# Gather of experts: the sample block as one tile of 64 rows, a 23rd weight block, a permuted product

## Chip, cores, metric

One core of a Trainium2 chip. The time is that of the device, in microseconds, from start to end of one execution; it is given as the median of three runs.

## What is computed

One layer of a decoder for a prompt of 512 tokens and a sample group of 8 x 4 = 32 tokens, in float32: attention, convolution and memory branches, their sum `x1`, and on it a mixture of 32 experts. Only that last part is touched:

```
def hier_moe(h, lw):
    ...
    gates = jnp.einsum('nk,nke->ne', w, jax.nn.one_hot(expert_ids, N_EXPERTS, dtype=jnp.float32)).astype(h.dtype)
    y = jnp.zeros_like(h)
    for e in range(N_EXPERTS):
        hid = jax.nn.silu(h @ lw['w_expert_gate'][e]) * (h @ lw['w_expert_up'][e])
        y = y + gates[:, e:e + 1] * (hid @ lw['w_expert_down'][e])
    return y
```

Each token goes to two of the 32 experts (the best group of 8, two experts in it). An expert's weights are 1024 x 512 (gate), 1024 x 512 (up) and 512 x 1024 (down).

## The kernel before

The branches and the output projection fill the first 710 us; nothing of them is changed. Then the router's result is turned into tables, and the experts follow one after the other, 0 to 31.

**Tokens.** They lie in five blocks `xts[0..4]` of 128 rows by 1024 columns: four of prompt rows, and block 4 with the 32 sample rows (copied there from `x1s`, 32 rows of which lie in each of four groups of partitions, lines 1136 to 1138) and zeros below. `posE` holds for each row and expert the place of the row in the expert's list, at most `CAP` = 64 rows; further ones go to a loop for overflow behind the 32 experts.

**Gather.** An expert's 64 rows are picked by matmuls with one-hot matrices (`gather`, line 1290). So that this can be done in float16, `to_halves` (line 1323) turns each block into a high half (ScalarE, `nc.scalar.mul`) and a low half (VectorE, the rest). A gather runs over 5 blocks x 2 halves x 2 halves of the columns, 20 matmuls. The result is copied by ScalarE to `xg` (line 1298), transposed in four pieces (line 1301) and scaled by VectorE into `xT1` (line 1302). Expert 0's input `xT0` is made ahead of the halves, in float32 (lines 1336 to 1353).

**An expert** (`expert_mm`, line 1471): gate and up products (line 1477, 32 matmuls each in the profile), behind them the gather for the next expert (`mid`), then silu on ScalarE, the product `hs` on VectorE (line 1486), two transposes of it, with columns taken in steps of two (line 1489), a copy to `hT` (line 1491), the down product (line 1495), the scaling by the gates (line 1498) and a scatter with addition by GpSimd (line 1499).

**Weights.** Each expert has six loads of 1024 KB: gate, gate, up, up, down, down. I number them 0 to 191; loads 6e to 6e + 5 belong to expert e. They are all issued in this order by SyncE's queue (`wload`, line 1430; line 573 in the profile), and load n also waits for load n - 4. Their blocks come in rounds from seven pools (`mraw`, line 1414): ring2 4, ring2b 2, ring2c 1, ring 6, ring3 5, ring4 2, ring5 2, so 22 in all:

```
        q = seq[0] % (RING + RING2 + RING2B + RING2C + RING3 + RING4 + RING5)
        for cand, n in ((ring2, RING2), (ring2b, RING2B), (ring2c, RING2C), (ring, RING), (ring3, RING3), (ring4, RING4), (ring5, RING5)):
```

Load n takes the block of load n - 22 and waits until the last matmul that reads it is over. The pool ring holds places 7 to 12 of each round, ring4 18 and 19, ring5 20 and 21; ring5 takes memory that the router's tables held.

**Overflow tables.** In the program behind expert 14's loads stands `overflow_tables` (line 1503). Its work memory `scr` is a block of the pool ring too, the next one in turn. In the fourth round, loads 66 to 87, ring holds loads 73 to 78; `scr` takes the block of load 73. Its instructions on VectorE begin at line 1522; line 1530 writes the number of overflow blocks, `novf`. The read of that number by the engines (line 1576) is written behind the last expert, but the scheduler, which orders every engine's instructions by times that it works out itself, puts SyncE's read between load 84 and load 85. SyncE's queue stops there until line 1530 is done.

Of the kernel before, what the change touches and what calls it, by code (L numbers as in the profile page):

```python
# [11 lines left out]
F32 = mybir.dt.float32  # L12
# [5 lines left out]
ALU = mybir.AluOpType  # L18
# [3 lines left out]
P = 128  # L22
D = 1024
NP = 512
NS = 32
# [11 lines left out]
CAP = 64  # L37
# [14 lines left out]
RING2B = 2  # L52
RING2C = 1
RING3 = 5
RING4 = 2
RING5 = 2
SPOS = 2
NPG = 2
# [95 lines left out]
def build(tc, I, O, cols):  # L154
    nc = tc.nc
# [25 lines left out]
    ident = cp.tile([P, P], F32, name="ident")  # L181
# [17 lines left out]
    def nm(s):  # L199
        cnt[0] += 1  # L200
        return f"{s}_{cnt[0]}"
# [593 lines left out]
    for b in range(DB):  # L795
# [14 lines left out]
        for h in range(4):  # L810
            r = slice(32 * h, 32 * h + 32)
            q = [qm[:, 4 * g + h, :] for g in range(3)]
            nc.tensor.matmul(psA[r], q[1], KT[h], start=False, stop=last, skip_group_check=True)
        for h in range(4):
            r = slice(32 * h, 32 * h + 32)
            q = [qm[:, 4 * g + h, :] for g in range(3)]
            nc.tensor.matmul(psB[r, 0:P], q[0], KT[h][:, 384:], start=False, stop=False, skip_group_check=True)
        for h in range(4):
            r = slice(32 * h, 32 * h + 32)
            q = [qm[:, 4 * g + h, :] for g in range(3)]  # L820
# [261 lines left out]
    rh = rt.tile([P, 5], F32, name="frh")  # L1082
# [13 lines left out]
    xts = {i: x_buf(i, [P, D], F32, "x1") for i in range(5)}  # L1096
    xst = ExitStack()
    xp = xst.enter_context(pool("xs", 1, side="right"))
    x1s = xp.tile([P, 256], F32, name="x1s")
# [47 lines left out]

    nc.vector.scalar_tensor_tensor(lg[:32, 4, :], pr[:32, 4, :], rss[:32], br_[:32], op0=ALU.mult, op1=ALU.add)
    nc.gpsimd.tensor_scalar(rh[:, 4:5], rs[:, 4:5], HS, None, op0=ALU.mult)

    def scores(ip):
        a = slice(2 * ip, 2 * ip + 2)
# [62 lines left out]
    V = nc.vector  # L1215
# [74 lines left out]
    def gather(oh, psum, xg, xT):  # L1290
        px = psum()
        for i in GORD:
            parts = halves_of[i]
            for r, src in enumerate(parts):
                for f in range(2):
                    nc.tensor.matmul(px[CAP * f:CAP * f + CAP], oh[:, i, :], src[:, 4 * f:4 * f + 4, :],  # L1296
                                     start=(i == GORD[0] and r == 0), stop=(i == GORD[-1] and r == len(parts) - 1))
        nc.scalar.copy(xg, px)
        pt = psum()
        for c in range(4):  # L1300
            mark = nc.tensor.transpose(pt[:, c * P:(c + 1) * P], xg[:, c * P:(c + 1) * P], ident)
        nc.vector.tensor_tensor(xT.rearrange("p (f c) s -> p c f s", f=2),
                                pt.rearrange("p (c f s) -> p c f s", c=4, f=2),
                                gE.rearrange("p (f c) -> p c f", f=2).unsqueeze(3).to_broadcast([P, 4, 2, CAP]),
                                op=ALU.mult)
        return mark
# [8 lines left out]
    work = h2pool.tile([P, 1184], F32, name="work")  # L1315
    for i in GORD:
        picked = V.tensor_scalar(oh0[i], cfs("iota64"), posE[:, i, 0:1], rh[:, i:i + 1], op0=ALU.is_equal, op1=ALU.mult)
    xT0 = h2pool.tile([P, 8, CAP], F32, name="xT0")
    def not_before(ins, other):
        tc.add_manual_dep(ins.ins, other.ins.name,  # L1320
                          mybir.DependencyInfo(mybir.DependencyClass.Sync, mybir.DependencyReason.DATA), reason="order")

    def to_halves(i, h2, act, dve):
        src = halves_of[i][0]
        for f in range(2):
            ks = slice(4 * f, 4 * f + 4)
            with tc.issue_after(act.ins):
                act = nc.scalar.mul(h2[:, 0, ks], src[:, ks], rh[:, i:i + 1])
            if i == 4 and not f:
                not_before(act, picked)  # L1330
            with tc.issue_after(dve.ins):
                V.scalar_tensor_tensor(h2[:, 1, ks], src[:, ks], rh[:, i:i + 1], h2[:, 0, ks],
                                       op0=ALU.mult, op1=ALU.subtract)
        return [h2[:, 0], h2[:, 1]]

    mark = counted
    for v in range(2):
        px = mm.tile([P, 2, P], F32, name=nm("mm"), tag="mm")
        for i in GORD:
            for f in range(2):  # L1340
                k = 4 * v + 2 * f
                with tc.issue_after(mark.ins):
                    got = nc.tensor.matmul(px[CAP * f:CAP * f + CAP], oh0[i], halves_of[i][0][:, k:k + 2, :],
                                           start=(i == GORD[0]), stop=(i == GORD[-1]))
        mark = got
        xv = xp.tile([P, 256], F32, name="xv") if v else xT0[:, 4:].rearrange("p k s -> p (k s)")
        copied = nc.scalar.copy(xv, px.rearrange("p a b -> p (a b)"))
        pt = tr.tile([P, 2, 2, CAP], F32, name=nm("tr"), tag="tr")
        for c in range(2):
            nc.tensor.transpose(pt[:, c].rearrange("p f s -> p (f s)"), xv[:, c * P:(c + 1) * P], ident)  # L1350
        ks = slice(4 * v, 4 * v + 4)
        taken = V.tensor_tensor(xT0[:, ks].rearrange("p (f c) s -> p c f s", f=2), pt,
                        gE[:, ks].rearrange("p (f c) -> p c f", f=2).unsqueeze(3).to_broadcast([P, 2, 2, CAP]), op=ALU.mult)

    for i in (4, 0, 1, 2, 3):
        shape = [P, 2, 8, P]
        h2 = h2pool.tile(shape, F16, name=nm("h2")) if i == 4 else x_buf((i - 1) % 5, shape, F16, "h2")
        halves_of[i] = to_halves(i, h2, counts if i == 4 else copied, taken)
    xgT = x_buf(3, [P, D], F32, "xgT")
# [111 lines left out]
    def expert_mm(xT, w, gc, idc2, mid, early):  # L1471
        pgt = pm.tile([P, 256], F32, name=nm("pg"), tag="pg")
        pup = pm.tile([P, 256], F32, name=nm("pu"), tag="pu")
        for ps, ws in ((pgt, w[0:2]), (pup, w[2:4])):
            for k in range(8):
                for f in range(2):
                    last = nc.tensor.matmul(ps[CAP * f:CAP * f + CAP], xT[:, k, :], ws[k // 4][:, k % 4, 256 * f:256 * f + 256],  # L1477
                                     start=(k == 0), stop=(k == 7))
            if early is not None and ps is pgt:
                early(last)  # L1480
        if mid is not None:
            with tc.issue_after(last.ins):
                mid()
        hs = work[:, 512:768]
        nc.scalar.activation(hs, pgt, AF.Silu)
        nc.vector.tensor_tensor(hs, hs, pup, op=ALU.mult)  # L1486
        ph = pm.tile([P, 2, P], F32, name=nm("ph"), tag="ph", bufs=1)
        for k in range(2):
            nc.tensor.transpose(ph[:, k, :], hs.rearrange("p (q k) -> k p q", k=2)[k], ident)
        hT = work[:, 768:1024].rearrange("p (f s) -> p f s", f=2)  # L1490
        nc.vector.tensor_copy(hT, ph)  # L1491
        pd = pm.tile([P, 512], F32, name=nm("pd"), tag="pd")
        for kk in range(4):
            for f in range(2):
                last = nc.tensor.matmul(pd[CAP * f:CAP * f + CAP], hT[:, kk % 2, CAP * (kk // 2):CAP * (kk // 2) + CAP],  # L1495
                                 w[4 + kk // 2][:, kk % 2, 512 * f:512 * f + 512], start=(kk == 0), stop=(kk == 3))
        o = work[:, :512]
        nc.vector.tensor_scalar(o, pd, gc, None, op0=ALU.mult)  # L1498
        nc.gpsimd.indirect_dma_start(out=y2, out_offset=bass.IndirectOffsetOnAxis(ap=idc2, axis=0), in_=o,  # L1499
                                     in_offset=None, compute_op=ALU.add)  # L1500
        return last
# [142 lines left out]
```

## Time and profile before

| | |
|---|---|
| median of 3 runs | 1222.54 us (1222.43 to 1224.62) |
| profiled execution | 1223.19 us, span 1221.4 us |
| TensorE busy | 1157.7 us, 95% |
| VectorE, ScalarE, GpSimd busy | 483.6, 303.0, 290.0 us |
| read from HBM, written | 295.66 MB, 31.35 MB |
| granted TensorE clock, mean | 0.992 |

The span runs from the first to the last instruction. Times in the trace count from its start. A matmul's time in the trace is from its start to its modelled end; matmuls overlap, so the busy time of a group is less than the sum of its instructions. The share of DMA is the mean over the core's 16 DMA engines.

### The profile page before, as it was taken

The numbers are of one execution on the slowest core, as the hardware profiler recorded it, in microseconds if no ns is written. First come the engines' busy times: TensorE is split into PE (matmuls) and PEld (weight loads), VectorE is DVE, ScalarE is ACT, GpSimd is POOL, SyncE is SP. The second block draws the span as 40 slices with busy tenths as digits, with TensorE's granted clock in tenths as the row PEclk, the third lists the DMA queues.
The fourth block names the chain that finished last, engine by engine and source line by source line (L and its number), as shares of the span: only waits on it lengthen the run. The fifth ranks groups of instructions, "written<-read, shape, count | busy, mean of one in ns | idle before, by whom it ended". The sixth has DMA issues, their size and how long they took to land. (4 is left out here: it accounts for less than half of the span.)

```text
span 1221.4 us, 22282 instructions
## 1 busy us (share of the span) xinstructions
PE 1157.7 (95%) x9250; PEld 853.9 (70%) x9250; DVE 483.6 (40%) x959; ACT 303.0 (25%) x731; POOL 290.0 (24%) x472
## 2 busy tenths in 40 slices
PE   6999999999999989999999997999999999888886
PEld 5898898989645889999998853555555555444442
DVE  6634444343534879946433254211133221111111
ACT  7434344423322422244332223000000000000000
POOL 4442434540740640212222000111111111001111
PEclk9999999999999989999999998999999999999998
DMA  9994754132656643313309477999999999999996
GB/s 321 233 333 118 251 155 163 45 110 104 209 169 226 224 123 103 104 36 104 139 6 404 164 289 273 395 405 404 404 378 384 406 402 406 404 403 404 403 404 241
DMA packets 117382, 313.02 MB, mean 256 GB/s; under 512 B 12841, under 2 KB 69489, under 8 KB 92448
## 3 DMA queue, kind: packets, MB, share of 16 engines
q1 hardware_dynamic: 107248, 295.58, 64.2%
q0 software_dynamic: 7280, 14.36, 5.3%
q10 hardware_dynamic: 2752, 1.65, 0.5%
q8 instruction: 74, 1.21, 0.4%
q14 instruction: 28, 0.23, 0.1%
HBM read 295.66 MB, written 31.35 MB: 268 GB/s over the span
## 5 line engine op out<-in xcount | busy, mean ns | idle before, releaser
L1499 POOL DMA_INDIRECT out_y_all<-work,ids x32 | 49.6, 1550 | 454.5 <-DVE work L1498 428.7
L664 PE MATMUL mm<-hTh,lo 128*128 128x272 f32 x512 | 148.5, 291 | 0.0
L663 PE MATMUL mm<-hTl,hi 128*128 128x272 f32 x512 | 148.4, 290 | 0.0
L662 PE MATMUL mm<-hTh,hi 128*128 128x272 f32 x512 | 148.3, 290 | 0.0
L1477 PE MATMUL pu<-w,xgT 128*64 128x256 f32 x992 | 115.3, 381 | 15.8 <-DMA w<-in_w_expert_up 14.5
L1495 PE MATMUL pd<-w,work 128*64 128x512 f32 x512 | 119.5, 609 | 1.0 <-DVE work L1491 0.5
L1477 PE MATMUL pg<-w,xgT 128*64 128x256 f32 x992 | 114.6, 380 | 2.4 <-DMA w<-in_w_expert_gate 1.2
L238 PE MATMUL mm<-hi,hTh 128*128 128x256 f32 x384 | 110.2, 287 | 0.0
L1477 PEld LDWEIGHTS pu<-w,xgT 128*64 128x64 f32 x992 | 69.3, 137 | 58.4 <-DMA w<-in_w_expert_up 23.6
L239 PE MATMUL mm<-lo,hTh 128*128 128x256 f32 x384 | 110.0, 286 | 0.0
L240 PE MATMUL mm<-hi,hTl 128*128 128x256 f32 x384 | 109.8, 286 | 0.0
L1477 PEld LDWEIGHTS pg<-w,xgT 128*64 128x64 f32 x992 | 70.3, 137 | 53.6 <-issue 16.0
L232 DVE TENSOR_TENSOR lo<-w,hi 128x2048 fp32r<-128x2048 f32 (+2 forms) x46 | 82.2, 1803 | 45.9 <-ACT hi L231 45.9
L662 PEld LDWEIGHTS mm<-hTh,hi 128*128 128x128 f32 x512 | 96.7, 189 | 1.8 <-ACT aS L896 0.8
L1486 DVE TENSOR_TENSOR work<-work,pu 128x256 f32<-128x256 f32 x32 | 13.5, 421 | 211.5 <-PE pu L1477 211.5
L663 PEld LDWEIGHTS mm<-hTl,hi 128*128 128x128 f32 x512 | 96.8, 189 | 0.3 <-issue 0.2
L664 PEld LDWEIGHTS mm<-hTh,lo 128*128 128x128 f32 x512 | 96.3, 189 | 0.6 <-issue 0.5
L683 DVE SCALAR_TENSOR_TENSOR cT<-u,cT 128x512 f32<-128x512 f32 x120 | 89.5, 763 | 1.7
L1495 PEld LDWEIGHTS pd<-w,work 128*64 128x64 f32 x512 | 34.4, 139 | 64.5 <-issue 60.6
L1296 PE MATMUL px<-h,ohs 128*64 128x512 f16 x620 | 74.0, 380 | 5.4 <-DVE gates L1373 2.8
L231 ACT CAST hi<-w 128x2048 fp32r<-128x2048 f32 (+2 forms) x50 | 68.1, 1391 | 27.8 <-PE mm L663 24.7
L999 POOL TENSOR_TENSOR z<-z,gth 128x272 f32<-128x272 f32 x32 | 35.7, 1117 | 164.0 <-DVE gth L998 164.0
(454 smaller groups left out, 2119.7 us busy)
## 6 DMA issues: line engine op xcount, KB each, us to landing
w<-in_w_expert_gate SPq DMA_DIRECT2D x64, 1024.0 KB, 11.1
w<-in_w_expert_up SPq DMA_DIRECT2D x64, 1024.0 KB, 10.3
w<-in_w_expert_down SPq DMA_DIRECT2D x64, 1024.0 KB, 11.1
w<-in_w_in SPq DMA_DIRECT2D x30, 512.0 KB, 7.1
w<-in_w_in SPq DMA_DIRECT2D x12, 1024.0 KB, 6.5
out_k_win_sample<-in_cache_k SPq DMA_DIRECT2D x8, 1016.0 KB, 12.9
out_v_win_sample<-in_cache_v SPq DMA_DIRECT2D x8, 1016.0 KB, 15.7
w<-in_cache_k SPq DMA_DIRECT2D x6, 1024.0 KB, 6.0
```

The source lines that it names most:

```text
L231: nc.scalar.copy(hi[:, s], v8(t)[:, s])
L232: last_lo[0] = e.tensor_tensor(lo[:, s], v8(t)[:, s], hi[:, s].bitcast(F32), op=ALU.subtract)
L238: nc.tensor.matmul(ps, xh[k], wh[k], start=(k == 0), stop=False)
L239: nc.tensor.matmul(ps, xh[k], wl[k], start=False, stop=False)
L240: nc.tensor.matmul(ps, xl[k], wh[k], start=False, stop=(k == n - 1))
L662: nc.tensor.matmul(ps, wh[k], xh[k], start=(k == 0), stop=False)
L663: nc.tensor.matmul(ps, wh[k], xl[k], start=False, stop=False)
L664: nc.tensor.matmul(ps, wl[k], xh[k], start=False, stop=(k == n - 1))
L683: nc.vector.scalar_tensor_tensor(cTf[:, c, :NP], u[:, c, j:j + NP], w, cTf[:, c, :NP], op0=ALU.mult, op1=ALU.add)
L1296: nc.tensor.matmul(px[CAP * f:CAP * f + CAP], oh[:, i, :], src[:, 4 * f:4 * f + 4, :], start=(i == GORD[0] and r == 0), stop=(i == GORD[-1 ...
L1477: last = nc.tensor.matmul(ps[CAP * f:CAP * f + CAP], xT[:, k, :], ws[k // 4][:, k % 4, 256 * f:256 * f + 256], start=(k == 0), stop=(k == 7))
L1495: last = nc.tensor.matmul(pd[CAP * f:CAP * f + CAP], hT[:, kk % 2, CAP * (kk // 2):CAP * (kk // 2) + CAP], w[4 + kk // 2][:, kk % 2, 512 * ...
```

## The change

Three edits.

1. The 32 sample rows stand twice in block 4, in rows 0 to 31 and 32 to 63 (four more copies from `x1s` on GpSimd's queue). `posE` of block 4 is copied to rows 32 to 63. Of the float16 tile of block 4, rows 0 to 31 hold the high halves and rows 32 to 63 the low halves, so its share of a gather is one pair of matmuls over 64 rows instead of two pairs over 128. Expert 0's own gather takes 32 rows of block 4.
2. ring4 has three blocks. `xT0` has no tile of its own any more: it lies in the first block of ring4, which becomes free when expert 0's gate and up products have read it. 23 weight blocks go round.
3. The product of silu and up is written permuted, the two groups of columns apart, into the 256 columns that held `hT`; `hT` is written where silu's result was. The transposes read contiguous columns.

```
-RING4 = 2
+RING4 = 3
...
     nc.gpsimd.tensor_scalar(rh[:, 4:5], rs[:, 4:5], HS, None, op0=ALU.mult)
+    for q in range(4):
+        nc.gpsimd.dma_start(xts[4][32:64, 256 * q:256 * q + 256], x1s[32 * q:32 * q + 32, :])
...
-                    nc.tensor.matmul(px[CAP * f:CAP * f + CAP], oh[:, i, :], src[:, 4 * f:4 * f + 4, :],
+                    nc.tensor.matmul(px[CAP * f:CAP * f + CAP], oh[:64 if i == 4 else P, i, :], src[:, 4 * f:4 * f + 4, :],
...
-    xT0 = h2pool.tile([P, 8, CAP], F32, name="xT0")
+    nc.vector.tensor_copy(posE[32:64, 4, :], posE[0:32, 4, :])
+    xT0 = ring4.tile([P, 2048], F32, name=nm("w"), tag="w")[:, :512].rearrange("p (k s) -> p k s", k=8)
...
+        a, b = (slice(0, 64), slice(32, 64)) if i == 4 else (slice(0, P), slice(0, P))
+        his = h2[a] if i == 4 else h2[:, 0]
+        los = h2[b] if i == 4 else h2[:, 1]
...
-                act = nc.scalar.mul(h2[:, 0, ks], src[:, ks], rh[:, i:i + 1])
+                act = nc.scalar.mul(his[:, ks], src[a, ks], rh[a, i:i + 1])
...
-                V.scalar_tensor_tensor(h2[:, 1, ks], src[:, ks], rh[:, i:i + 1], h2[:, 0, ks],
+                V.scalar_tensor_tensor(los[:, ks], src[b, ks], rh[b, i:i + 1], h2[b, ks] if i == 4 else his[:, ks],
                                        op0=ALU.mult, op1=ALU.subtract)
-        return [h2[:, 0], h2[:, 1]]
+        return [his] if i == 4 else [his, los]
...
-                    got = nc.tensor.matmul(px[CAP * f:CAP * f + CAP], oh0[i], halves_of[i][0][:, k:k + 2, :],
+                    rows = slice(0, NS if i == 4 else P)
+                    got = nc.tensor.matmul(px[CAP * f:CAP * f + CAP], oh0[i][rows], halves_of[i][0][rows, k:k + 2, :],
...
-        nc.vector.tensor_tensor(hs, hs, pup, op=ALU.mult)
+        hp_ = work[:, 768:1024].rearrange("p (k q) -> p k q", k=2)
+        nc.vector.tensor_tensor(hp_.rearrange("p k q -> p q k"), hs.rearrange("p (q k) -> p q k", k=2),
+                                pup.rearrange("p (q k) -> p q k", k=2), op=ALU.mult)
...
-            nc.tensor.transpose(ph[:, k, :], hs.rearrange("p (q k) -> k p q", k=2)[k], ident)
-        hT = work[:, 768:1024].rearrange("p (f s) -> p f s", f=2)
+            nc.tensor.transpose(ph[:, k, :], hp_[:, k], ident)
+        hT = hs.rearrange("p (f s) -> p f s", f=2)
```

The scheduler and the pools make more of this than the diff shows. In the rows that follow a name's number is that of its tile, `w` are weight blocks (and `scr`), DMAHW counts the landings of loads, and the lines are those of the program the rows are from.

On SyncE's queue, loads 18 to 23, before:

```order
L573 DMA w_8602<-in_w_expert_gate 128x2048 [waits DMAHW1_49,Pool_49]
L573 DMA w_8604<-in_w_expert_gate 128x2048 [waits DMAHW4_49]
L573 DMA w_8606<-in_w_expert_up 128x2048 [waits DMAHW5_49]
L573 DMA w_8608<-in_w_expert_up 128x2048 [waits DMASW3_49,DMASW4_49,DMASW2_49,DMASW5_49,DMASW1_49,DMASW6_49,DMASW0_49,DMASW7_49,DVE_49,DMAHW2_49,PE_49,DMAHW6_49,Activation_49,Pool_49]
L573 DMA w_8610<-in_w_expert_down 128x2048 [waits DMAHW7_49,DMAHW3_49,PE_49]
L573 DMA w_8612<-in_w_expert_down 128x2048 [waits DMAHW0_49,PE_49]
```

and in the change:

```order
L573 DMA w_8601<-in_w_expert_gate 128x2048 [waits DMAHW1_49,Pool_49]
L573 DMA w_8603<-in_w_expert_gate 128x2048 [waits DMAHW4_49]
L573 DMA w_8605<-in_w_expert_up 128x2048 [waits DMAHW5_49,DVE_49,PE_49]
L573 DMA w_8607<-in_w_expert_up 128x2048 [waits DMAHW6_49,DMAHW2_49]
L573 DMA w_8609<-in_w_expert_down 128x2048 [waits DMASW5_49,DMASW4_49,DMASW6_49,DMASW3_49,DMASW7_49,DMASW2_49,DMAHW3_49,DMASW1_49,DMAHW7_49,DMASW0_49,Pool_49]
L573 DMA w_8611<-in_w_expert_down 128x2048 [waits DMAHW0_49]
```

Load 20, the first up load of expert 3, waits for TensorE now, and loads 21 to 23 stand behind it.

On VectorE, around the first instructions of the overflow tables, before (`pd` scaled in the first row is expert 11's, the product in the last is expert 12's):

```order
L1498 TENSOR_SCALAR work<-pd_9419,gates 128x512 [waits DMASW0_49,DVE_49,PE_49]
L1522 TENSOR_TENSOR w_9626<-cn,cf 128x256 [waits DMAHW2_49,DMAHW6_49,DMAHW0_49,PE_49]
...
L1530 CAST novf<-w_9626 128x1 [waits DVE_49]
L1531 TENSOR_TENSOR w_9626<-w_9626 128x32
L1533 TENSOR_TENSOR w_9626<-OH,w_9626 128x320 [waits DVE_49]
L1486 TENSOR_TENSOR work<-work,pu_9443 128x256 [waits PE_49,Activation_49]
```

and in the change (again from the scaling of expert 11 on; line 1494 is the product, 1500 the copy to `hT`, 1304 the gathered input, 1507 the scaling, 1531 the first instruction of the tables, 1539 the count):

```order
L1507 TENSOR_SCALAR work<-pd_9400,gates 128x512 [waits DMASW4_49,PE_49]
L1494 TENSOR_TENSOR work<-work,pu_9424 128x128x2 [waits PE_49,Activation_49]
L1286 TENSOR_TENSOR ohs<-posE,cf 128x320 [waits PE_49]
L1500 COPY work<-ph_9486 128x256 [waits DVE_49,PE_49]
L1304 TENSOR_TENSOR xgT_8266<-px_9478,gE 128x4x2x64 [waits PE_49]
L1531 TENSOR_TENSOR w_9603<-cn,cf 128x256 [waits DMAHW2_49,DMAHW3_49,DMAHW1_49,PE_49]
...
L1507 TENSOR_SCALAR work<-pd_9490,gates 128x512 [waits DMASW5_49,PE_49]
...
L1539 CAST novf<-w_9603 128x1 [waits DVE_49]
```

The tables stand behind four instructions of expert 12 that they stood ahead of, and expert 12's scaling stands among them, ahead of the count. SyncE's read of the count stands between loads 84 and 85 in both.

## Rows read from the trace of the kernel before

**Rows 1.** The page: the span, and the DMA line of its 40 slices.

```profile
span 1221.4 us, 22282 instructions
...
DMA  9994754132656643313309477999999999999996
```

**Rows 2.** Windows: stretch, length, busy us of PE, PEld, DVE, ACT, POOL, clock, DMA share, GB/s.

```profile
756.00:906.00 150.00, 146.72 (x1138) 80.82 (x1134) 29.19 (x54) 10.69 (x22) 15.48 (x10) 1.00 1.02 399
921.00:1030.00 109.00, 106.92 (x853) 59.37 (x850) 22.55 (x51) 7.19 (x15) 12.36 (x8) 1.00 1.02 402
1030.00:1200.00 170.00, 150.68 (x1102) 76.18 (x1104) 28.66 (x52) 10.31 (x21) 16.52 (x11) 1.00 1.02 406
```

**Rows 3.** Waits from 1030 us on: us in total, times, longest.

```profile
PE pu L1477 <- DMA w<-in_w_expert_up: 14.5, 20, 1.7
```

**Rows 4.** Timeline of the last expert's down product: start, us, engine, line.

```profile
1210.67 1.94 PE L1495 MATMUL pd<-w,work 128*64 128x512 f32 x8 [0.42 <-DMA w<-in_w_expert_down]
```

**Rows 5.** Timeline of SyncE's queue: loads 20 and 21, 22 and 23, 24 and 25, 26.

```profile
716.57 3.27 SPq L573 DMA_DIRECT2D w<-in_w_expert_up  x2
730.28 2.06 SPq L573 DMA_DIRECT2D w<-in_w_expert_down  x2
734.42 2.06 SPq L573 DMA_DIRECT2D w<-in_w_expert_gate  x2
749.71 2.64 SPq L573 DMA_DIRECT2D w<-in_w_expert_up  x2
```

**Rows 6.** Windows at the start of the experts.

```profile
720.00:760.00 40.00, 33.59 (x226) 15.92 (x224) 18.51 (x33) 13.90 (x16) 1.74 (x1) 0.91 0.73 267
744.00:750.80 6.80, 6.11 (x17) 1.80 (x17) 2.42 (x4) 1.02 (x2) 0.00 (x0) 0.51 0.05 8
```

**Rows 7.** Timeline of SyncE's queue: loads 84 and 85, and load 85 alone.

```profile
905.98 10.04 SPq L573 DMA_DIRECT2D w<-in_w_expert_gate  x2
...
915.69 0.34 SPq L573 DMA_DIRECT2D w<-in_w_expert_gate  x1
```

**Rows 8.** Waits of SyncE's queue, 900 to 920 us.

```profile
SPq L1576 <- DVE w L1531: 8.5, 1, 8.5
```

**Rows 9.** Windows: from load 84's issue to its landing.

```profile
906.00:917.40 11.40, 11.40 (x96) 6.50 (x92) 6.41 (x26) 0.56 (x2) 1.54 (x1) 1.00 0.85 314
```

**Rows 10.** Timeline of TensorE: expert 1's gate; expert 12's gate, gather, transposes, down product.

```profile
753.43 3.67 PE L1477 MATMUL pg<-w,xgT 128*64 128x256 f32 x32 [0.87 <-DVE xgT L1302]
...
907.90 3.62 PE L1477 MATMUL pg<-w,xgT 128*64 128x256 f32 x32
...
914.80 2.33 PE L1296 MATMUL px<-h,ohs 128*64 128x512 f16 x20
...
917.87 0.66 PE L1301 MATMUL px<-ident,xgT 128*128 128x128 f32 x4 [0.30 <-ACT xgT L1298]
918.56 3.65 PE L1495 MATMUL pd<-w,work 128*64 128x512 f32 x16
```

**Rows 11.** Timeline of GpSimd: the last of the four copies of x1s.

```profile
654.91 0.50 POOL L1138 DMA_DIRECT2D x<-x1s  x1 [1.85 <-DMA out_y_all<-x]
```

**Rows 12.** Timeline of VectorE: the overflow tables up to the count, expert 12's scaling.

```profile
911.57 0.43 DVE L1522 TENSOR_TENSOR w<-cn,cf 128x256 f32<-128x256 f32 x1 [2.70 <-PE pg L1477]
...
914.01 0.17 DVE L1527 COPY w<-w 128x8 f32<-128x8 f32 x1
...
914.59 0.15 DVE L1530 CAST novf<-w 128x1 int32<-128x1 f32 x1
...
922.39 0.74 DVE L1498 TENSOR_SCALAR work<-pd,gates 128x512 f32<-128x512 f32 x1
```

**Rows 13.** DMA issues, KB, us to landing: load 26, load 84, load 85, each in a window of its own.

```profile
w<-in_w_expert_up SPq DMA_DIRECT2D x1, 1024.0 KB, 5.0
w<-in_w_expert_gate SPq DMA_DIRECT2D x1, 1024.0 KB, 11.4
w<-in_w_expert_gate SPq DMA_DIRECT2D x1, 1024.0 KB, 5.4
```

More of the change, by code (lines that the diff above doesn't have):

```diff
@@ L1355, in build @@
     for i in (4, 0, 1, 2, 3):
-        shape = [P, 2, 8, P]
+        shape = [P, 8, P] if i == 4 else [P, 2, 8, P]
         h2 = h2pool.tile(shape, F16, name=nm("h2")) if i == 4 else x_buf((i - 1) % 5, shape, F16, "h2")
```

## The prediction

> **What bounds the kernel now.** I read the page first: the span and the DMA line of the forty slices [rows 1]. From about 760 us on the DMA digit is 9 almost everywhere, while TensorE too looks full. The windows tell the two apart [rows 2]: from 756 to 906 us TensorE is busy 146.72 of 150 us and the DMA share is 1.02; from 1030 to 1200 us the share is still 1.02, but TensorE is down to 150.68 of 170 us. The waits of that late stretch name what it lacks: up-weights, 20 waits [rows 3]. So TensorE starts with a stock of weights loaded ahead, uses it up until about 1030 us, and then lives from hand to mouth. All through this the weight stream is the bound, and the last load sets the end: the second half of the last down product begins at 1210.67 us, released by its load, and only 1.94 us of matmuls, a scaling and one scatter follow [rows 4]. **A gain on TensorE is therefore worth nothing by itself; only what stops or restarts the weight stream counts.** It stops in two places, and I read both.
>
> The first is the start. With 22 blocks, loads 20 and 21 go out at 716.57 us; load 22 needs the block of expert 0's first gate half and goes at 730.28, loads 24 and 25 need its up halves (734.42, the second at about 736.2), load 26 its first down half (749.71) [rows 5]. Between these the stream runs dry: 8 GB/s in 744 to 750.8 us, and 267 GB/s over 720 to 760 us, so 10.7 MB moved [rows 6].
>
> The second is in the middle. SyncE's queue issues load 84 at 905.98 us and load 85 only at 915.69 [rows 7]. The waits say why: 8.5 us for VectorE, at the read of the overflow count (L1576), which stands in the queue between loads 84 and 85 [rows 8]. In this stretch the DMA share is 0.85 [rows 9]: 0.15 x 11.4 us = 1.7 us are lost even now.
>
> **Part by part.** *One tile of 64 rows for the sample.* Each gather loses 2 of its 20 matmuls, which take 2.33 us together [rows 10]: 0.233 us. The rest of the cycle keeps its length: TensorE waits 0.30 us for ScalarE's copy before the transposes [rows 10], and that copy starts when the gather ends, so all of it shifts. From expert 1's gate at 753.43 to expert 12's at 907.90 us the cycle is 154.47 / 11 = 14.04 us; it becomes 13.81. Behind the weight stream this is worth nothing, but it brings forward, by 12 x 0.233 = 2.8 us, the moment of expert 12's down product, which is needed below. The conversion to halves keeps its instructions (fewer partitions, the same 512 columns), so I leave the start of expert 1 where it is. The copy of 32x32 positions on VectorE lies in the gap in which VectorE waits for the first gather. The four added x1s copies on GpSimd take about 0.50 us each [rows 11], behind waits for earlier copies to land; rh and the sample's logits follow some 3 us later, but VectorE now takes the logits two instructions later, so nothing waits. Without that cover it would be the same 3 us, once, on a stretch in which TensorE is full. They add 0.13 MB at a time when the stream has a dry spell ahead of it.
>
> *The permuted product.* The transposes read contiguous columns. They stand between the gather and the 0.30 us wait for ScalarE [rows 10], so what they save lengthens that wait: nothing. The product itself runs under the gather of the next expert (2.10 us after the change); only above that would it show, and then behind the weight stream.
>
> *The 23rd block at the start.* Expert 0's input lies in the first block of ring4, so load 20 now waits for expert 0's last up matmul, about 736.2 us, with loads 21 and 22 behind it although ring5 is free. The stream is dry from about 723 us (loads 20 and 21 no longer fill 723 to 728). But then seven loads (20 to 26) may go at once, and the next block falls free at 749.7, before they are done: the dry spell of 744 to 750.8 is gone. Moved by 760 us: 3 us before 723, and from 737.4 (the issue and 1.2 us) 22.6 us, at 406 GB/s [rows 2]: 10.4 MB against 10.7. That is 0.3 MB, 0.7 us: no difference, within one us either way, and it doesn't reach the end, since the second stop absorbs it.
>
> *The 23rd block in the middle: the term that decides.* The overflow tables (L1522 to L1530, then L1531 on) work in a block taken from ring, the next in its turn. Their first instruction waited for the last reader of load 73, half of expert 12's gate, and ran at 911.57 us, when that gate product ended [rows 12]. With 23 blocks the round of four begins at load 69 instead of 66, ring's six places hold loads 76 to 81, and the block next in turn is that of load 76: expert 12's first down half. The order of VectorE's instructions shows it too: product, transposed copy and gathered input of expert 12 now stand ahead of the first table instruction, and the scaling of expert 12's down product stands between it and the count. SyncE's read of the count has kept its place, ahead of load 85. So:
> - expert 12's down product starts at 918.56 - 2.8 = 915.8 us and is half done after 3.65 / 2 us [rows 10]: 917.6 us, the first table instruction;
> - twelve instructions, 911.57 to 914.01 before [rows 12], 2.44 us: 920.0 us. The down product is over by then (919.4), so the scaling (0.74 us) ends at 920.8 us;
> - the last five up to the count, 914.01 to 914.59 + 0.15 = 914.74 before: 921.5 us;
> - from the count's end to load 85's issue it was 915.69 - 914.74 = 0.95 us: **922.4 us**.
>
> By then the four loads in flight have landed (load 84 took 11.4 us from 905.98, so 917.4) and the queue is empty. A load into an empty queue landed after 5.0 us (load 26) and load 85 itself after 5.4 [rows 13]. So load 85 lands at 922.4 + 5.0 = 927.4 us instead of 915.69 + 5.4 = 921.1: **+6.3 us**. [...]
>
> From there the stream is full again as before, and every later load and the end move by the same amount. TensorE can't win it back: its stock is smaller, so it meets the stream some experts after 12 and not at 1030 us.
>
> **The sum.** PE gain 0, start 0 (absorbed), middle +6.3. The profiled execution took 1223.19 us with a span of 1221.4 and lies 0.65 above the median of 1222.54, so 1229.5 on its scale and **1228.8 us** as a median. Bounds: if TensorE's cycle lost the 0.30 us wait as well, the count came 3.6 us earlier: +2.7, 1225.2. If the 2.8 us of TensorE don't come: +9.1, 1231.6. That gives 1225.0 to 1232.0.
>
> **Rivals.**
> - *The table's start is not pushed back, and the change is not slower.* Then the count comes 2.8 us earlier than before, SyncE no longer stops long enough to empty the stream, and the 1.7 us come back: 1220.8 us. It decides at a count ready by about 916 us. For it: only the 2.8 us. Against: the block's number and the order agree. 0.12.
> - *The gather doesn't get shorter*, because the pair with 64 rows was never the costly part: +9.1, 1231.6 us. 0.10.
> - *The block counts in full*: the stream is one load ahead, 1024 KB at 406 GB/s, 2.6 us, on top of the first rival: 1218.2 us. It needs load 20 not to be held up by expert 0's input. 0.04.
> - *The clock falls.* TensorE now waits for weights from some experts after 12 on instead of from 1030 us. From 1030 to 1200 us, with such waits, the granted clock was 1.00, the 2.4 GHz level [rows 2]; at the 1.2 GHz level, as granted for most of 744 to 750.8 us [rows 6], the last 1.94 us of matmuls [rows 4] would take twice that: 1230.7 us. 0.03. [...]
>
> **How the numbers follow.** The forecast keeps 0.71. A measurement of this kernel tells about 0.2% from no change, 2.4 us: 1220.1 to 1225.0. Slower: forecast, second and fourth rival, 0.84. Same: most of the first, 0.10. Faster: the third and a little of the first, 0.06. The range of 1225.0 to 1232.0 holds the cases that make up 0.84.
>
> **What the profile after would show.** Right: SyncE waits some 15 us instead of 8.5 at the read of the count; load 85 goes at 921 to 924 us; the first table instruction is released by a down product; the page's DMA digit falls for one slice near 920 us; no dry spell at 744 to 750 but one from 723 to 737 us; a cycle of 13.8 us before 900 us; waits of TensorE for weights well before 1030 us. Wrong: a count ready before 917 us, or a load 85 less than 3 us later than it was; then the middle term is gone and the first rival holds.

## The result, and the profile after

The changed kernel takes **1232.99 us** (median of 4 runs, 1231.98 to 1233.46) where the kernel before takes 1222.53 (1222.43 to 1224.62): a ratio of 1.008, 95% interval 1.0063 to 1.0098. It is slower, by 10.5 us. The forecast was 1228.8 us with 1225.0 to 1232.0: the right side, but 4.2 us short, and the time lies 1.0 us above the range. The profiled execution took 1233.43 us, with a span of 1231.6.

The page after, its span and the DMA line of the forty slices. The slices are 30.8 us long; the 7 among the 9s is 893 to 924 us and marks the stop:

```profile
span 1231.6 us, 22137 instructions
...
DMA  9895654132747542313319359999979999999996
```

The windows after (stretch, length, busy us of PE, PEld, DVE, ACT, POOL, clock, DMA share, GB/s). The first answers to [rows 9], the last two to [rows 6]:

```profile
906.00:917.40 11.40, 11.40 (x94) 6.11 (x92) 1.54 (x3) 0.38 (x1) 1.54 (x1) 1.00 0.86 330
917.40:925.00 7.60, 7.23 (x50) 3.38 (x48) 5.04 (x20) 0.58 (x1) 0.22 (x1) 1.00 0.01 1
921.00:1030.00 109.00, 101.53 (x768) 51.41 (x766) 30.67 (x81) 6.78 (x14) 10.80 (x7) 1.00 0.97 379
...
720.00:760.00 40.00, 33.98 (x218) 15.13 (x216) 19.38 (x34) 14.05 (x16) 1.74 (x1) 0.87 0.65 261
744.00:750.80 6.80, 6.26 (x16) 1.71 (x17) 3.07 (x4) 1.68 (x2) 0.00 (x0) 0.50 1.01 422
```

From 917.4 to 925 us nothing is loaded: 1 GB/s. Before, 906 to 917.4 us was the worst of it, with a share of 0.85 [rows 9]. From 921 us on TensorE is busy 101.53 of 109 us where it had been busy 106.92 [rows 2]. It now waits for up-weights already between 921 and 1030 us, as forecast, where before it waited for none there (us in total, times, longest):

```profile
PE pu L1484 <- DMA w<-in_w_expert_up: 4.3, 7, 0.8
```

The waits of SyncE's queue, the one at the read of the count (us in total, times, longest), which was 8.5 us [rows 8]:

```profile
SPq L1585 <- DVE w L1540: 18.1, 1, 18.1
```

SyncE's timeline (start, us, engine, line; a row of x2 holds two loads): loads 20 and 21, 22 and 23, 84 and 85, load 85 alone, load 191:

```profile
736.71 0.80 SPq L573 DMA_DIRECT2D w<-in_w_expert_up  x2
737.87 1.04 SPq L573 DMA_DIRECT2D w<-in_w_expert_down  x2
...
906.86 19.59 SPq L573 DMA_DIRECT2D w<-in_w_expert_gate  x2
...
926.11 0.34 SPq L573 DMA_DIRECT2D w<-in_w_expert_gate  x1
...
1209.99 0.33 SPq L573 DMA_DIRECT2D w<-in_w_expert_down  x1
```

Load 85 goes out at 926.11 us and not 915.69 [rows 7]: 10.42 us later. Load 191, the last, goes at 1209.99 and had gone at 1199.56: 10.43 us later. So what delays load 85 makes the whole loss in this run: the last load moves by as much.

VectorE's timeline: the first instruction of the overflow tables, the scaling that stands among them, the count:

```profile
921.43 0.43 DVE L1531 TENSOR_TENSOR w<-cn,cf 128x256 f32<-128x256 f32 x1 [1.19 <-PE pd L1504]
...
923.76 0.74 DVE L1507 TENSOR_SCALAR work<-pd,gates 128x512 f32<-128x512 f32 x1
...
925.02 0.15 DVE L1539 CAST novf<-w 128x1 int32<-128x1 f32 x1
```

The releaser is the one that the prediction named, a down product, and the scaling lies inside. But all of it is 3.7 to 3.8 us later than forecast (917.6 for the first instruction, 921.5 for the count's end). TensorE's timeline says why: expert 1's gate, then expert 12's gate, up, gather, the transposes of the product and those of the gathered rows:

```profile
754.09 3.67 PE L1484 MATMUL pg<-w,xgT 128*64 128x256 f32 x32 [0.87 <-DVE xgT L1304]
...
908.87 3.62 PE L1484 MATMUL pg<-w,xgT 128*64 128x256 f32 x32
912.32 3.62 PE L1484 MATMUL pu<-w,xgT 128*64 128x256 f32 x32
915.87 2.25 PE L1298 MATMUL px<-h,ohs 64*64 64x512 f16 x18
918.05 0.44 PE L1498 MATMUL ph<-ident,work 128*128 128x128 f32 x2
918.86 0.66 PE L1303 MATMUL px<-ident,xgT 128*128 128x128 f32 x4 [0.37 <-ACT xgT L1300]
```

And before, expert 12's up product and the transposes of its product:

```profile
911.35 3.62 PE L1477 MATMUL pu<-w,xgT 128*64 128x256 f32 x32
...
917.06 0.50 PE L1489 MATMUL ph<-ident,work 128*128 128x128 f32 x2
```

The cycle of an expert, from one gate product to the next, is (908.87 - 754.09) / 11 = 14.07 us, against 14.04 before and 13.81 forecast. The gather has 18 matmuls and no longer 20, yet from the up product's start to the first transpose it is 918.05 - 912.32 = 5.73 us, against 917.06 - 911.35 = 5.71 before. **The 2.8 us that TensorE was to bring forward did not come.** Where they went shows in the weight loads (PEld) at the seams, the places where matmuls of 128 rows and of 64 rows follow one another. After, then before:

```profile
915.87 0.11 PEld L1298 LDWEIGHTS <-ohs 64*64 64x64 f16 x2 [0.39 <-issue]
916.21 1.44 PEld L1298 LDWEIGHTS <-ohs 128*64 128x64 f16 x16 [0.23 <-issue]
```

```profile
914.59 2.06 PEld L1296 LDWEIGHTS <-ohs 128*64 128x64 f16 x20
```

Before, the first one-hot was loaded at 914.59 us, under the up product's last matmuls, 0.21 us ahead of its own matmul at 914.80 [rows 10]. After, the weights of 64 rows load at 915.87, at the start of their own matmul, with 0.39 us of idle PEld ahead, and the next ones, for 128 rows again, idle 0.23 us first. This gave the theory for the runs: **the loss is the queue stopped at the read, because the tables sit in a down block; and the pair of 64 rows gives back at its two seams what the pair left out had saved.** The rivals: part of the loss lies at the start, in the strided product, or in the gather itself; or the 23rd block does harm of another kind.

### The profile page after: what moved, and what is told of

The parts are those of the page before. It is cut to its first block, busy times and chain, and to the rows that moved or that the text cites. A ratio compares the mean times of both kernels' runs of the same rounds, so it can differ in the third digit from the quotient of the medians.

```text
span 1231.6 us, 22137 instructions
## 1 busy us (share of the span) xinstructions
PE 1160.9 (94%) x9186; PEld 841.6 (68%) x9188; DVE 489.5 (40%) x960; ACT 302.2 (25%) x731; POOL 291.7 (24%) x476
## 5 line engine op out<-in xcount | busy, mean ns | idle before, releaser
L1494 DVE TENSOR_TENSOR work<-work,pu 128x256 f32<-128x256 f32 x32 | 19.5, 608 | 220.8 <-PE pu L1484 220.8
L1298 PE MATMUL px<-h,ohs 64*64 64x512 f16 (+1 forms) x558 | 72.2, 387 | 5.0 <-DVE gates L1380 2.9
```

The source lines that it names most:

```text
L1298: nc.tensor.matmul(px[CAP * f:CAP * f + CAP], oh[:64 if i == 4 else P, i, :], src[:, 4 * f:4 * f + 4, :], start=(i == GORD[0] and r == 0), ...
```

## The experiments

Ten kernels ran, each against the kernel before on its own chip. That kernel's median there was 1222.83 us (19 runs, the first four), 1222.79 (27, the next four) and 1222.48 (15, the last two). Load 0 goes out at 639.4 to 641.9 us in the twelve profiles, ahead of anything that the change touches. So beside the times I give for each the stretch from the issue of load 0 to that of load 191 in its one profile, which leaves this scatter out.

| kernel | time, us | load 85, us | load 0 to load 191, us | cycle, us |
|---|---|---|---|---|
| before | 1222.53 | 915.69 | 559.32 | 14.04 |
| change | 1232.99 | 926.11 | 569.53 | 14.07 |
| pair over 128 rows | 1230.41 | 922.56 | 566.04 | 13.83 |
| pair of 64 rows last | 1232.72 | 924.64 | 567.93 | 13.95 |
| product as before | 1232.72 | 925.87 | 569.32 | 14.07 |
| before, tables wait | 1227.08 | (load 87: 926.01) | 563.43 | 14.04 |
| 22 blocks | 1225.87 | 915.41 | 561.92 | 14.07 |
| 22 blocks, read held | 1222.71 | 915.24 | 559.43 | 14.07 |
| tables in a gate block | 1223.32 | 917.63 | 560.26 | 14.07 |
| late read | 1222.45 | 908.35 | 558.04 | 14.07 |
| before, late read | 1222.96 | 910.54 | 558.09 | 14.04 |
| all together | 1222.40 | 909.37 | 558.77 | 13.87 |

**The pair over all 128 rows.** In the change:

```diff
-                    nc.tensor.matmul(px[CAP * f:CAP * f + CAP], oh[:64 if i == 4 else P, i, :], src[:, 4 * f:4 * f + 4, :],
+                    nc.tensor.matmul(px[CAP * f:CAP * f + CAP], oh[:, i, :], src[:, 4 * f:4 * f + 4, :],
...
+        if i == 4:
+            nc.gpsimd.memset(h2[64:], 0.0)
...
-        return [his] if i == 4 else [his, los]
+        return [h2] if i == 4 else [his, los]
```

> The change with the sample's pair over all 128 rows (the lower 64 rows of its tile set to zero once): 18 matmuls in the gather, all with 128 rows. Theory (the pair of 64 rows costs about two changes of the number of rows in use, 0.10 us going in and 0.12 coming out, as much as the pair left out saved): the cycle falls from 14.07 to 13.83 +- 0.04 us, the first gather matmul follows the up product by 0.21 and not 0.31 us, the next pair by 0.22 and not 0.335; expert 12's down product and with it the count come 2.4 to 2.9 us earlier, load 85 is issued at 923.5 +- 0.5, and the time is 1230.4 +- 0.7 us. Rival (the gain of the gather is given back elsewhere, in the wait for the copy or the transposes): cycle 14.0 to 14.07, time 1232.5 to 1233.5.

Measured: 1230.41 us (1229.44 to 1231.19; ratio 1.0064, 1.0047 to 1.008). TensorE's timeline, expert 1's gate and expert 12 up to the transposes, and SyncE's row of load 85:

```profile
753.46 3.67 PE L1486 MATMUL pg<-w,xgT 128*64 128x256 f32 x32 [0.87 <-DVE xgT L1304]
...
905.55 3.62 PE L1486 MATMUL pg<-w,xgT 128*64 128x256 f32 x32
909.01 3.62 PE L1486 MATMUL pu<-w,xgT 128*64 128x256 f32 x32
912.46 2.11 PE L1298 MATMUL px<-h,ohs 128*64 128x512 f16 x18
914.50 0.44 PE L1500 MATMUL ph<-ident,work 128*128 128x128 f32 x2
```

```profile
922.56 0.34 SPq L573 DMA_DIRECT2D w<-in_w_expert_gate  x1
```

From up to gather it is 3.45 us, as before (911.35 to 914.80); in the change it is 3.55. From gather to transposes it is 2.04 us; in the change 2.18, before 2.26. So the way into 64 rows costs 0.10 us and the way out of them 0.14, together 0.24, and the matmuls left out save 0.22: with the same 18 matmuls, only the rows changed, 0.24 us per expert come back, 13.83 against 14.07. Load 85 then goes at 922.56 us, where the prediction had put it at 922.4. The cycle and the time are the theory's, load 85 goes 0.4 us ahead of its range, and the rival (given back elsewhere) falls.

**The pair of 64 rows last.** In the change, the gather's order for the blocks:

```diff
-        for i in GORD:
+        for i in (0, 1, 2, 3, 4):
...
```

> The change with the sample's pair of 64 rows as the last of the gather's nine pairs, not the first. Theory (0.10 us going to 64 rows and 0.12 us coming back to 128 are what ate the pair left out): if the way back falls together with the wait ahead of the transposes that follow, only 0.10 us is left, the cycle is 13.95 +- 0.03 us, load 85 is issued 1.3 us earlier and the time is 1231.6 +- 0.7 us; if the way back is paid at the transposes, the cycle stays at 14.05 to 14.08 and the time at 1232.5 to 1233.5. Rival (not the change of rows costs, but the place right behind the up product): the cycle falls to 13.83 and the time to 1230.4.

```profile
910.96 3.62 PE L1484 MATMUL pu<-w,xgT 128*64 128x256 f32 x32
914.41 2.23 PE L1298 MATMUL px<-h,ohs 128*64 128x512 f16 x18
916.58 0.44 PE L1498 MATMUL ph<-ident,work 128*128 128x128 f32 x2
```

From up to gather it is 3.45 us again; from gather to transposes it is 2.17 against 2.04 without any seam, so 0.13 us remain (0.12 by the cycle, 13.95 against 13.83), about what the way in costs: most of the way back has fallen together with what comes ahead of the transposes. Cycle and load 85 (924.64, 1.47 us earlier) are the theory's, and neither of the others'. The median, 1232.72 us (1231.58 to 1233.44), is not: it lies 0.4 us above the theory's range and in that of the case in which the way back is paid. It does not show the 1.5 us; the stretch does, 567.93 against 569.53.

**The product in its old order.** In the change:

```diff
-        hp_ = work[:, 768:1024].rearrange("p (k q) -> p k q", k=2)
-        nc.vector.tensor_tensor(hp_.rearrange("p k q -> p q k"), hs.rearrange("p (q k) -> p q k", k=2),
-                                pup.rearrange("p (q k) -> p q k", k=2), op=ALU.mult)
+        nc.vector.tensor_tensor(hs, hs, pup, op=ALU.mult)
...
-            nc.tensor.transpose(ph[:, k, :], hp_[:, k], ident)
-        hT = hs.rearrange("p (f s) -> p f s", f=2)
+            nc.tensor.transpose(ph[:, k, :], hs.rearrange("p (q k) -> k p q", k=2)[k], ident)
+        hT = work[:, 768:1024].rearrange("p (f s) -> p f s", f=2)
```

> The change without its third edit: the product written in its old order, read with a stride by the transposes. Theory (the permuted product is hidden under the gather, and what the transposes save goes into the wait for the copy): VectorE's product 0.42 and not 0.61 us, the transposes' pair 0.50 and not 0.44, the cycle 14.05 to 14.15 us, time 1233.2 +- 0.8 us. Rival A (the permuted product delays the transposes, and the chain with them): cycle 13.9 or less, time 1230.5 to 1232. Rival B (the permuted product had been a gain hidden by a worse gather): cycle 14.2 or more, 1234 to 1236.

Measured: 1232.72 us (1232.3 to 1234.28), cycle 14.07. Groups of instructions by line, the product on VectorE, of this run and of the change:

```profile
L1493 DVE TENSOR_TENSOR work<-work,pu 128x256 f32<-128x256 f32 x32 | 13.5, 421 | 220.4 <-PE pu L1484 220.4
```

```profile
L1494 DVE TENSOR_TENSOR work<-work,pu 128x256 f32<-128x256 f32 x32 | 19.5, 608 | 220.8 <-PE pu L1484 220.8
```

The third edit makes the product 0.19 us dearer (421 to 608 ns) and the transposes 0.06 cheaper (0.50 to 0.44), and neither reaches the cycle.

**The kernel before, with the tables' wait alone.** The first instruction of the tables waits for the first half of expert 12's down product:

```diff
+            if kk == 1:
+                downs.append(last)
...
-        V.tensor_tensor(cmp_, cn.unsqueeze(2).to_broadcast([P, 32, 8]),
+        first_op = V.tensor_tensor(cmp_, cn.unsqueeze(2).to_broadcast([P, 32, 8]),
...
+        not_before(first_op, downs[12])
```

> The kernel before (22 blocks, 20 matmuls, product as it was) with one wait added: the first operation of the overflow tables waits for the first half of expert 12's down product, as the block of load 76 makes it wait in the change. The read of the count then stands behind load 86 and not 84. Theory (the wait alone makes the loss): the count comes near 924.5 to 925.5, load 87 is issued near 926 and not before; two more loads (2.7 us each) have gone out ahead of the stop than in the change, so the loss is 10.4 less 5.4: 1222.5 + 5 = 1227.5, range 1226 to 1230. Rival (the late tables alone don't cost, the loss needs the 23rd block or another edit): 1222 to 1224 us.

Measured: 1227.08 us (1225.69 to 1228.82; ratio 1.0033, 1.0022 to 1.0045). VectorE's first table instruction, and SyncE's loads 84 and 85, 86 and 87:

```profile
921.92 0.43 DVE L1524 TENSOR_TENSOR w<-cn,cf 128x256 f32<-128x256 f32 x1 [1.19 <-PE pd L1495]
```

```profile
907.66 2.80 SPq L573 DMA_DIRECT2D w<-in_w_expert_gate  x2
912.63 13.72 SPq L573 DMA_DIRECT2D w<-in_w_expert_up  x2
```

Loads 85 and 86 go out in time, load 87 at 926.01. None of the three edits is in this kernel, and the one wait, with two more loads ahead of the stop, makes 4.1 us of the stretch (563.43 against 559.32) where 5 were expected; the time lies in the expected range.

**22 blocks.** The change without its second edit:

```diff
-RING4 = 3
+RING4 = 2
...
-    xT0 = ring4.tile([P, 2048], F32, name=nm("w"), tag="w")[:, :512].rearrange("p (k s) -> p k s", k=8)
+    xT0 = h2pool.tile([P, 8, CAP], F32, name="xT0")
```

> The change without its second edit: 22 weight blocks and the first expert's input in a tile of its own again, but the sample's pair of 64 rows and the permuted product stay. Theory (all of the loss is the queue of the loads, stopped by the count's read, because the 23rd block gives the overflow tables the block of a down half; the other two edits cost and gain nothing at the end): as before the change, 1222.5 +- 1 us, load 85 issued within 1 us of 915.7, the cycle of an expert 14.0 to 14.1 us. Rival A (the pair of 64 rows or the permuted product costs time by itself, at the end or on VectorE): 1225 to 1233 us. Rival B (the start, where the first expert's input shares no block): 1222.5 less 0 to 1 us.

Measured: 1225.87 us (1224.75 to 1227.85; ratio 1.0027, 1.0015 to 1.0038). This is 2.4 us beyond the theory's bound and falls, by its number, to rival A. SyncE's load 83, then load 84:

```profile
902.35 0.33 SPq L573 DMA_DIRECT2D w<-in_w_expert_down  x1
...
914.98 0.34 SPq L573 DMA_DIRECT2D w<-in_w_expert_gate  x1
```

The order of the queue had moved: the read stands ahead of load 84 here, so one load more was held up. Whether that is all of it, or the two edits cost something, the next run decides.

**22 blocks, the read held behind load 84.** As the last, and:

```diff
-    n_ovf = nc.values_load(novf[0:1, 0:1], min_val=0, max_val=MAXOVF)
+    with tc.issue_after(loads[84]):
+        n_ovf = nc.values_load(novf[0:1, 0:1], min_val=0, max_val=MAXOVF)
```

> As the run with 22 blocks, but the read of the count is held where both kernels had it, behind load 84 (in that run it had gone ahead of load 84, which then was issued at 914.98 and not near 906). Theory (the 3 us of that run are one load that was held up more, and the pair of 64 rows and the permuted product cost nothing at the end): load 84 issued near 905, load 85 at 915.4 +- 0.4, time 1222.8 +- 0.8 us, cycle 14.07. Rival (the 3 us came from the gather or the product): 1225 to 1227 us.

Measured: 1222.71 us (1222.3 to 1224.58; ratio 1.0002, 0.9992 to 1.0011), load 85 at 915.24 us. So with the read where it stood the first and the third edit cost nothing at the end; the loss comes in with the second, and the first only sets how large it is (1230.41 us with the pair over 128 rows). One load more or less behind the read is 561.92 - 559.43 = 2.5 us.

**The tables in a gate block.** The whole change, 23 blocks, with the tables in the next block of another ring, that of load 73, and the read held behind load 84:

```diff
-        scr = ring.tile([P, 2048], F32, name=nm("w"), tag="w")
+        scr = ring2b.tile([P, 2048], F32, name=nm("w"), tag="w")
```

> The whole change with 23 blocks, but the overflow tables take the block of load 73 (the second gate half of expert 12) from another ring, and the read of the count is held behind load 84. Theory (the 23rd block costs only by which load's block it hands to the tables): the tables' first operation at 911 to 912, the count at 914.5 +- 0.7, load 85 issued at 916 +- 0.8, time 1223.2 +- 1.0 us. Rival (23 blocks cost also by what they do to the stream, or to the loads' order): 1226 to 1233 us.

Measured: 1223.32 us (1222.67 to 1225.11; ratio 1.0006, 0.9997 to 1.0015). The tables' first instruction, and SyncE's wait at the read, which are those of before again [rows 12, 8]:

```profile
913.52 0.43 DVE L1531 TENSOR_TENSOR w<-cn,cf 128x256 f32<-128x256 f32 x1 [2.70 <-PE pg L1484]
```

```profile
SPq L1586 <- DVE w L1540: 8.5, 1, 8.5
```

In this profile everything from load 0 on is 1.4 us later than before (641.61 against 640.24), so 913.52 and load 85's 917.63 stand for 912.2 and 916.3. One name in one line, with the read held where it stood anyway, takes back some 9.7 us: the 23rd block costs by which load's block it hands to the tables.

**The late read.** The change, with the read behind the last load:

```diff
+    with tc.issue_after(loads[-1]):
+        n_ovf = nc.values_load(novf[0:1, 0:1], min_val=0, max_val=MAXOVF)
```

> The change, with the read of the count put behind the last weight load in SyncE's queue; nothing else differs. Theory: the tables still start late, but no load waits for them; the 18.1 us wait at the read and the empty stretch 917.4 to 925 vanish, load 85 follows load 84 by what its block allows, and the time is 10.4 us less, and the 1.7 us less that the kernel before lost at the same place too: 1221 us, range 1219.5 to 1222.8. Rival A (part of the loss lies elsewhere: the start, the gather, the strided product): 1224 to 1231. Rival B (with 23 blocks never stopped the stream runs ahead of all, and the bound goes to TensorE): below 1219.

Measured: 1222.45 us (1221.62 to 1222.97; ratio 0.9996, 0.9987 to 1.0006). The two windows that were 0.86 and 0.01:

```profile
906.00:917.40 11.40, 11.22 (x94) 6.03 (x90) 1.87 (x4) 0.84 (x2) 1.54 (x1) 1.00 1.03 398
917.40:925.00 7.60, 7.42 (x52) 3.88 (x54) 5.71 (x23) 0.13 (x1) 1.50 (x1) 1.00 1.02 429
```

The tables are as late as in the change (first instruction at 920.16 us), but no load waits for them, and the loss is gone. The time lies in the expected range, though 1.4 us above the 1221 us that counted on winning back what the kernel before loses at its own stop.

**The kernel before with the late read.** The same edit in the kernel before.

> The kernel before with the read of the count behind the last load: 22 blocks that never stop. Theory (a 23rd block is worth nothing once the stream runs, since the start is bound by expert 0's up product, which frees the blocks; the stop at load 85 costs what it leaves the transfer engines empty, 1.7 us by the windows): 1221 to 1222.6 us, the same within 0.1% as 23 blocks with the late read (1222.45). Rival (the 23rd block is worth about a load of 2.5 us): 1224 to 1225.5.

Measured: 1222.96 us (1221.93 to 1225.67; ratio 1.0002, 0.9993 to 1.0011), 0.4 us above the expected range. The stretch is 558.09 us, with 23 blocks 558.04: the 23rd block is worth nothing once the stream is not stopped. Against the kernel before the stretch is 1.2 us shorter, but the times don't show it; the interval lets it be 0.9 us at most, so how much of the 1.7 us is won in the median stays open.

**All together.** 23 blocks, the pair over 128 rows, the tables in the block of load 69 (`ring2`), the read last.

> All that the runs call for at once: 23 blocks, the sample's pair over 128 rows, the overflow tables in an up block of expert 11 (load 69), the read of the count behind the last load. Theory (past the stop the stream of loads alone sets the end, so the cycle of 13.83 us is worth nothing there): load 85 issued near 908, the transfer engines full from 756 to the last load, time 1222.2 +- 0.8 us, the same as 23 blocks with the late read alone (1222.45) and not to be told from the kernel before. Rival (a shorter cycle frees blocks sooner, and the stream follows): 1218 to 1220.5.

Measured: 1222.40 us (1221.82 to 1224.44; ratio 0.9997, 0.9988 to 1.0006). Load 85 goes at 909.37 us, 1.4 us later than expected. From 1030 us on TensorE is busy less and the stream no faster:

```profile
906.00:917.40 11.40, 11.04 (x96) 6.54 (x94) 6.74 (x21) 0.97 (x2) 1.85 (x1) 1.00 1.02 394
1030.00:1200.00 170.00, 147.23 (x1078) 73.27 (x1076) 28.77 (x49) 9.68 (x20) 16.95 (x11) 1.00 1.02 404
```

With the late read alone TensorE was busy 151.23 of these 170 us, at 405 GB/s. The version beats the change by 10 us and is not to be told from the kernel before; no version here is faster than that kernel beyond its interval. Two things weren't tried: the second edit alone, and 23 blocks with a tile of its own for the first expert's input, which could fill the dry spell of 723 to 737 us.

## Why the prediction was wrong

**What bounds the kernel: right.** The end moved by as much as load 85 did (10.43 and 10.42 us). Taking the stop away gave it back, and a TensorE that was 0.2 us faster per expert gave nothing by itself (1222.40 us with everything together, 1222.45 with the late read alone).

**The gather: the step that failed.** "Each gather loses 2 of its 20 matmuls, which take 2.33 us together: 0.233 us." Taken per matmul this is about right: 0.22 us when all rows are in use. But I costed the pair that stayed as one of the nine, and never asked what lies at its seams. It takes 0.10 us to come into 64 rows and 0.14 to leave them, so the term was -0.03 us and not +0.233 per expert. Their whole worth, 2.8 us, lay in when expert 12's down product, and with it the tables, would start. The loss at the last load was 10.4 us and not 6.3. Of these 4.1 us, 3.7 lie between the forecast's load 85 (922.4) and the measured one (926.11), and 0.4 is the credit for a quicker landing (see the middle, below). Of the 3.7, 2.8 are the saving that didn't come; 11 x 0.03 = 0.3 are the two seams' excess over the saving; the last 0.66 is expert 1's gate, 754.09 against 753.43. Of that, 0.22 is the scatter (load 0 at 640.46 against 640.24), 0.10 comes between the two experts (24.6 to 25.5 us from gate to gate in the twelve profiles), and 0.34 is the same mistake once more, where I had left "the start of expert 1 where it is": expert 0's gather now takes 32 rows for the sample's block, the first block in each of its two passes. TensorE's last block of the first pass and the start of the second pass; after, then before:

```profile
722.00 1.10 PE L1350 MATMUL mm<-x,cf 128*64 128x256 f32 x4
723.04 4.00 PE L1350 MATMUL mm<-x,wr 32*64 32x256 f32 x16
```

```profile
721.70 1.10 PE L1343 MATMUL mm<-x,cf 128*64 128x256 f32 x4
722.62 3.87 PE L1343 MATMUL mm<-x,wr 128*64 128x256 f32 x16
```

The weight loads (PEld) of the second pass, from the sample's block to the next; after, then before:

```profile
723.04 0.19 PEld L1350 LDWEIGHTS mm<-x,wr 32*64 32x64 f32 x4 [0.87 <-issue]
...
724.08 0.20 PEld L1350 LDWEIGHTS mm<-x,wr 128*64 128x64 f32 x4 [0.85 <-issue]
```

```profile
722.62 0.16 PEld L1343 LDWEIGHTS mm<-x,wr 128*64 128x64 f32 x2 [0.30 <-issue]
...
723.54 0.16 PEld L1343 LDWEIGHTS mm<-x,wr 128*64 128x64 f32 x2 [0.30 <-issue]
```

Into the sample's block it is 1.04 us (722.00 to 723.04) and had been 0.92; out of it, to the next, it is 1.04 us and had been 0.92 for the same four matmuls. With the way out in the first pass these are three seams of 0.12 us, 0.36 in all. And expert 0's first gate comes 88.39 to 88.46 us behind load 0 in all nine kernels that have this edit, 88.05 to 88.06 in the three that don't.

In the run with 128 rows for the experts from 1 on, where the term is what I took it for, load 85 came within 0.2 us of the forecast (0.4 if counted from load 0) and the time, 1230.41, lay in the range, 1.6 us above the forecast.

**The permuted product: right.** It costs VectorE 0.19 us, under a gather that leaves 2 us, and nothing at the end.

**The 23rd block at the start: right.** 261 GB/s over 720 to 760 us are 10.4 MB, as worked out, and the dry spell of 744 to 750.8 became 422 GB/s, with one of 12 GB/s in 723 to 737 us instead. Four loads went at once there and not seven, since each also waits for the one four ahead of it; the sum is the same. From load 0 to load 84 it takes 266.4 to 266.5 us with 23 blocks, 265.7 to 266.2 with 22 (where the read doesn't stand ahead of load 84): 0.2 to 0.8 us, and the forecast had 0.7.

**The middle: right in mechanism.** The block of load 76, the releaser, the scaling among the tables, the 0.95 us from count to load (0.94): all as forecast. The credit of 0.4 us, for a landing of load 85 after 5.0 us where it had been 5.4, was not borne out in the change, where the last load moved by as much as load 85. Nor did load 85 land quicker in the run with 128 rows, where three more loads went out within 2 us behind it (KB, us to landing):

```profile
w<-in_w_expert_gate SPq DMA_DIRECT2D x1, 1024.0 KB, 6.2
```

Yet there the last load did move by 0.4 us less than load 85's issue (6.50 and 6.87). What part of a stop the stream makes good behind it stays open.

**The rivals.** The first and the third needed a count ready by about 916 us; it was ready at 925.2. The second, the gather that doesn't get shorter, gave 1231.6 us and is what happened, 1.4 us from it, but not for the reason that I gave it: the pair was as costly as any, and what leaving out the other saved, 0.22 us, was spent again at the seams. A chance of 0.10 was too little for a row that no trace had shown: matmuls of 64 rows between matmuls of 128. The clock did not fall: 1.00 in both windows from 921 to 1200 us, with more waits than before.

## What to carry to other kernels

A matmul that was left out saved its time here only where the ones around it kept their number of rows: look at the seam for a weight load that is no longer done ahead. When a ring grows by a block, find what else takes blocks from that rotation, and whose block it gets now. And a queue that feeds the bound should not hold a read of another engine's result among its loads; each load more that stood behind the read cost 2.5 us here.

## What the runs showed of the hardware

Weights for 128 rows loaded under a running matmul of 128 rows: the row of PEld before shows the first one-hot at 914.59 us, under the up product. Weights for 64 rows behind a matmul of 128 did not, and neither did those for 128 behind 64: 0.39 and 0.23 us of idle PEld, and 0.10 and 0.14 us on TensorE's path. The Trainium skill, in "TensorE: Matmul & The Clock Gate", section "The mechanism" of Part 3, names two cases in which a weight load is pulled ahead of running matmuls, a row group that doesn't conflict and the background weight buffer; a list in the same section says that the two overlap "only when row_grp differs". The rows of 128 behind 128 disagree with the list as it stands; whether the buffer of the other sentence is the reason, no run here shows.

The product of 128x256, its columns written in turn into two halves (the change), took 608 ns, and 421 written in order (the product as before). The transposes of 128x128 that read every second column (the product as before) took 334 ns each, those that read in order (the change) 301.
